# The order of five engine queues: paced by hand in the program, or recorded first and set by a list schedule

## The chip, the cores and the metric

One core of one Trainium2 chip runs the whole program. The metric is the device time of one execution in microseconds (us); lower is better. A program on one core is timed in several executions, and the median is given.

## The reference

Two transformer layers and one second block work on 512 tokens of width 1024, all in float32. Cut to what matters:

```python
for l in range(DEPTH):                       # 2 layers
    mod = silu(c) @ w_ada[l] + b_ada[l]      # shifts, scales, gates
    h = rms_norm(x, norm_mix[l]) * (1 + sc1) + sh1
    proj = h @ w_in[l]
    # delta rule: conv of 4 taps, silu, 8 heads of 128, chunks of tokens:
    #   solve (I + L) X = [v, k], then a scan over the chunks
    # window attention: 16 query heads on 2 key heads, blocks of 128 tokens
    merged = sigmoid(gate_a) * (o_dn @ w_dn_out[l]) + sigmoid(gate_b) * (o_swa @ w_swa_out[l])
    x = x + gt1 * (merged @ w_o[l])
    h = rms_norm(x, norm_ffn[l]) * (1 + sc2) + sh2
    a, b = split(h @ w_up[l])
    x = x + gt2 * ((silu(causal_dwconv(a)) * b) @ w_down[l])
# second block: band attention, a state space model, gates, a last norm
```

## The kernel before

**Products.** Each large product (`gemm_f`, `gemm_t`) reads its weights in chunks of 512 KB by SyncE's queue into `raw` (L238, three buffers). `split` makes a high part `whi` on ScalarE (L127) and a low part `wlo` on VectorE (L116), and TensorE multiplies three times in fp32r: high by high, high by low, low by high. These products write PSUM tiles named `gf` (features on partitions) or `gt` (tokens on partitions), of which there are four. A product is one matmul of 128x512.

**Chains.** Beside the products run chains of small steps with many waits between engines. A delta chain (`delta_chain`, one for each pair of heads, four in a layer) starts from `gram`, the products of keys with keys and queries, which VectorE scales into `ua`. `substitute` inverts the blocks of 16: SyncE writes `nd` to DRAM in eight DMAs, reads `pn`, VectorE runs 15 steps of a product `xt` and a sum `xi`, and the result goes out as `xd` and comes back as `xq` on other partitions. `inverse` builds the larger blocks with small matmuls on TensorE (`yps`, `zps`, `wps`) and VectorE's updates of `xf` and `wf`. A scan over four chunks follows (`kqs`, `xps`, `osps`; the state is `st`), and `delta_out` transposes the output (`otr`). A window chain (`swa_chain`, two in a layer) makes keys (`ktr`), queries (`qtr`), scores (`sc`), transposed weights (`ptr`) and values (`pvo`). `conv` runs a causal convolution on VectorE (`cacc`), whose result `qk` is transposed on TensorE (`qktr`). Part of the products by masks (`um`, `rg`) runs on GpSimd, named POOL. The second block has band chains and a state space chain of the same kind.

**What sets the order.** The chains are generators. After each three matmuls of a product `tick` adds to a credit, and for each PACE = 4 of credit `stage` advances the first chain by one step. Fixed numbers of empty steps hold a chain back until other engines are done: GAP = 6 after the substitution, OGAP = 8 before the output, WGAP, SGAP and BGAP in the others.

```python
def tick(self, n):
    self.credit += n
    while self.credit >= self.pace:
        self.credit -= self.pace
        self.stage()
```

`SEQ` names the order of a layer's parts: `F0 C0 F1 Z0 O0 C1 F2 ...`, with F for a pair's products, C for its chain, Z for gates, O for the output, Q and W for the window attention. The builder then orders what is written once more by its own rules, and hands out buffers in that order. Each engine runs its queue in order; a wait at the head holds all that stands behind.

Of the kernel before, what the change touches and what calls it, by code (L numbers as in the profile page):

```python
# [23 lines left out]
# matrix products of the gemms per stage of a chain, and the stages a chain waits for results of the other engines  # L24
PACE = 4
GAP = 6
OGAP = 8
WGAP = 1
SGAP = 7
BGAP = 3  # L30
# the order of a mixing layer's parts: delta rule heads by pairs (F products, C chain, Z gates, O output),
# window attention by key heads (Q queries, W attention)
# [7 lines left out]
# columns of the packed constants  # L40
# [4 lines left out]
# columns of the second block's packed per-feature vectors  # L45
W_GB, W_BG, W_D, W_AR, W_AI, W_DT, W_NG, W_N = 0, 16, 24, 28, 44, 60, 76, 84
# columns of a layer's packed per-feature vectors
# [4 lines left out]
# packed rows of a layer  # L52
R_QN, R_KN, R_SINK, R_ALOG, R_DTB, R_N = 0, 64, 128, 144, 152, 160


class Net:
    def __init__(self, ctx, tc, io, dbg=None):
        self.tc, self.nc, self.io, self.dbg = tc, tc.nc, io, dbg or {}
        nc = tc.nc
        self.V, self.A, self.G, self.PE, self.SP = nc.vector, nc.scalar, nc.gpsimd, nc.tensor, nc.sync  # L60
# [20 lines left out]
        self.sides = []  # L81
        self.chains, self.credit, self.pace = [], 0, PACE
# [124 lines left out]
    def rsqrt(self, out, x, n, scale, eps, name, on_pool=False):  # L207
        """out = (x * scale + eps) ** -0.5, out [128, n]"""
# [22 lines left out]
    def chunk(self, parts, kk, n, eng=None):  # L231
        """rows of kk x 128, n columns from the parts (dram views [kk * 128, n_i])"""
        raw = self.p_raw.tile([128, 1024], F32, name="raw", tag="raw")
        v = raw[:, :kk * n].rearrange("p (k c) -> p k c", k=kk)
        o = 0
        for w in parts:
            c = w.shape[1]
            self.SP.dma_start(out=v[:, :, o:o + c], in_=w.rearrange("(k p) c -> p k c", p=128))  # L238
            o += c
        hi, lo = self.split(raw, kk * n, eng)  # L240
        self.step()
        return self.views(hi, lo, kk, n)
# [6 lines left out]
    def gemm_f(self, w, c0, act, consume, ntile=2, parts=None, split=False):  # L249
        """features on partitions: tiles of 128 columns of w from c0; act: list of (hi, lo) [128, 512];  # L250
        split: the tokens' first half first"""
        kt = len(act)
        for g in range(ntile // 2):
# [11 lines left out]
            def mms(k0, n, hi, lo, ts):  # L265
                for ct in range(2):
                    o = slice(ct * 128, ct * 128 + 128)
                    for k in range(n):
# [4 lines left out]
                        self.tick(3)  # L273
# [12 lines left out]
    def gemm_t(self, parts, act, consume, step=2, last=2):  # L286
        """tokens on partitions: all columns of the parts (dram views [K, n_i]); act as in gemm_f;
        last: how many of the loads are gone through tile by tile"""
# [5 lines left out]
        def mms(t, k0, m, hi, lo):  # L294
            o = slice(t * 128, t * 128 + 128)
            for k in range(m):
# [4 lines left out]
                self.tick(3)  # L301
# [36 lines left out]
    def chain(self, gen, side=False):  # L338
        """a chain that runs after the ones before it; side: beside them"""
        (self.sides if side else self.chains).append(gen)  # L340

    def advance(self, gens, gen):
        with self.on("x"):
            try:
                next(gen)
            except StopIteration:
                gens.remove(gen)

    def stage(self):
        if self.chains:  # L350
            self.advance(self.chains, self.chains[0])
        for g in list(self.sides):
            self.advance(self.sides, g)

    def tick(self, n):
        self.credit += n
        while self.credit >= self.pace:
            self.credit -= self.pace
            self.stage()

    def flush(self):
        while self.chains or self.sides:
            self.stage()

# [1 line left out]
    def ada_acc(self, l, part):  # L366
        """sums over the rows of w_ada, still by partitions"""
# [12 lines left out]
    def ada_col(self, l, part, acc, q):  # L380
        """half q of the part as a column per 128 features: shifts, and norm * (1 + scale)"""
# [18 lines left out]
    def mod_gate(self, l, part):  # L400
        """a gate's row to dram (the first times a fourth)"""
# [15 lines left out]
    def row(self, name, src, lane="x"):  # L417
        """a row of dram on all partitions"""
# [13 lines left out]
    def norm_scale(self, ss):  # L432
        """1 / rms, a column, from both halves' sums of squares over D"""
# [5 lines left out]
    def norm_half(self, xn, t, q, a, b, h):  # L439
        """half q of the features of the scaled rows xn [128, 512], times a plus b, as hi and lo of h"""  # L440
# [24 lines left out]
    def first_norm(self, x0):  # L465
        """the modulation and norm before the first layer, a quarter of the features after the other"""
# [11 lines left out]
        def apply(q, acc):  # L478
# [3 lines left out]
            for part in range(2):  # L482
# [3 lines left out]
            self.tc.keep_in_program_order(  # L486
                self.tt(d, ps, self.vec[:, 0, V_ADA:V_ADA + 16].rearrange("p (a k) -> p a k", a=2)[:, :, f2], ADD))
# [45 lines left out]
    def conv(self, l, ps, ti, out):  # L533
        """causal conv of 4 taps along tokens, then 2 * silu"""
# [10 lines left out]
    def dn_scalars(self, l, hact):  # L545
        """k, v of the window attention and the delta rule's decays and betas"""
# [47 lines left out]
    def decays(self, b):  # L594
        """between the tokens of a chunk"""
# [14 lines left out]
    def delta_front(self, l, b, hact):  # L610
        """heads 2b, 2b + 1"""
# [52 lines left out]
        # v, token-major and scaled  # L664
# [27 lines left out]
    def delta_chain(self, l, b, qk, ua, kd, vk, sig):  # L692
        dn = self.dn
        xq = self.substitute(ua)
        for _ in range(GAP):
            yield
        tt_ = yield from self.inverse(ua, xq)
        # scan over the chunks
# [60 lines left out]
    def delta_out(self, l, b, ot, sz, odn):  # L759
        for _ in range(OGAP):  # L760
            yield
# [932 lines left out]
```

## Time and profile before

| | us |
|---|---|
| three runs | 2508.03, 2505.99, 2504.11 |
| median | 2505.99 |
| span of the profiled execution, first to last instruction | 2505.6 |
| TensorE busy in it | 2390.4 |
| VectorE, ScalarE, POOL busy | 1675.6, 1019.1, 520.1 |

The profile gives one time for the profiled execution, its span. In it PE is TensorE's matmuls and PEld its weight loads, DVE is VectorE, ACT ScalarE, SP SyncE. A matmul's end is modelled, so the distance from start to start of two matmuls tells more of the pace than the duration of one. The granted clock is a share of 2.4 GHz.

### The profile page before, as it was taken

What the parts mean: (1) busy time and instruction counts of PE and PEld (TensorE: products, weight loads), DVE (VectorE), ACT (ScalarE), POOL (GpSimd) and SP (SyncE); (2) the same over time, 40 slices, a digit from 0 to 9 for tenths busy, and PEclk for the clock granted to TensorE, in tenths of its full rate; (3) what the DMA queues carried; (4) which work ended last, traced back from release to release, by engine and by line L of the source; (5) the groups of instructions that cost most, each with busy time, mean ns of one, the idle gap of its engine ahead of it and who ended that gap; (6) DMA issues with size and microseconds to landing.
All of it is one profiled execution on the core that took longest, in us unless ns stands there. A gap on an engine that the chain in (4) does not pass through costs nothing.

```text
span 2505.6 us, 35740 instructions
## 1 busy us (share of the span) xinstructions
PE 2390.4 (95%) x13324; PEld 1939.6 (77%) x13324; DVE 1675.6 (67%) x3078; ACT 1019.1 (41%) x2095; POOL 520.1 (21%) x738
## 2 busy tenths in 40 slices
PE   6899898999999999999998989999999999999998
PEld 5677676778888888787777767888888888877786
DVE  6787788766576667478877976356646655855554
ACT  5444353642253233364434535234332334255432
POOL 2321314210500000113213241041005341600000
PEclk9999999999999999999999999999999999999999
DMA  8222223356365556442222223345533344632242
GB/s 260 71 64 63 70 72 100 118 173 223 122 202 172 171 172 196 131 125 72 57 63 64 78 70 114 112 146 179 157 113 114 103 140 156 204 115 76 82 137 76
DMA packets 239741, 309.09 MB, mean 123 GB/s; under 512 B 32144, under 2 KB 189712, under 8 KB 239568
## 3 DMA queue, kind: packets, MB, share of 16 engines
q1 hardware_dynamic: 228864, 275.64, 36.1%
q0 software_dynamic: 10416, 30.91, 3.5%
q8 instruction: 105, 1.72, 0.3%
q14 instruction: 68, 0.56, 0.1%
q10 hardware_dynamic: 288, 0.26, 0.0%
HBM read 276.20 MB, written 30.56 MB: 122 GB/s over the span
## 4 chain that ended last, share of the span: by engine, by line
PE 64%; DVE 7%; ACT 2%; issue 2%; DMA 2%; POOL 1%; SPq 0%; DVEq 0%; POOLq 0%; ACTq 0%
PE gf L130 41%; PE gt L130 15%; DVE wlo L116 1%; DVE xt L116 1%; ACT whi L127 1%; DMA raw<-in_w_ada_dram 1%; DVE cacc L119 1%; PE pvo L130 1%; PE bo L130 1%; PE sc L130 0%; DVE xi L788 0%; PE osps L130 0%; PE bs L130 0%; PE gram L130 0%; PE ntr L133 0%
## 5 line engine op out<-in xcount | busy, mean ns | idle before, releaser
L130 PE MATMUL gf<-hhi,whi 128*128 128x512 f32 (+1 forms) x1888 | 728.7, 387 | 5.1 <-ACT hhi L127 3.2
L130 PE MATMUL gf<-hlo,whi 128*128 128x512 f32 (+1 forms) x1888 | 725.7, 385 | 2.7 <-DVE hlo L116 2.7
L130 PE MATMUL gf<-hhi,wlo 128*128 128x512 f32 (+1 forms) x1888 | 724.5, 384 | 0.7 <-DVE wlo L116 0.6
L116 DVE TENSOR_TENSOR wlo<-raw,whi 128x1024 fp32r<-128x1024 f32 (+1 forms) x358 | 462.1, 1291 | 314.7 <-ACT whi L127 313.1
L127 ACT ACTIVATE whi<-raw 128x1024 fp32r<-128x1024 f32 (+1 forms) x366 | 378.3, 1036 | 631.2 <-PE gf L130 290.5
L130 PEld LDWEIGHTS gf<-hhi,whi 128*128 128x128 f32 x1888 | 359.7, 191 | 68.1 <-ACT hhi L127 4.0
L130 PEld LDWEIGHTS gf<-hlo,whi 128*128 128x128 f32 x1888 | 360.5, 191 | 62.8 <-DVE hlo L116 4.3
L130 PEld LDWEIGHTS gf<-hhi,wlo 128*128 128x128 f32 x1888 | 360.4, 191 | 62.0 <-DVE wlo L116 2.0
L130 PE MATMUL gt<-whi,g 128*128 128x512 f32 x704 | 219.5, 392 | 0.0
L130 PE MATMUL gt<-whi,hhi 128*128 128x512 f32 (+1 forms) x416 | 158.3, 381 | 5.0 <-ACT beta L127 2.7
L130 PE MATMUL gt<-whi,hlo 128*128 128x512 f32 (+1 forms) x416 | 157.6, 379 | 0.0
L130 PE MATMUL gt<-wlo,hhi 128*128 128x512 f32 (+1 forms) x416 | 157.5, 379 | 0.0
L130 PEld LDWEIGHTS gt<-whi,g 128*128 128x128 f32 x704 | 132.3, 189 | 27.2 <-issue 0.2
L130 PE MATMUL gt<-wlo,g 128*128 128x512 f32 x352 | 137.7, 391 | 0.0
L119 DVE SCALAR_TENSOR_TENSOR acc<-raw,csil,acc 128x1024 f32<-128x1024 f32 x70 | 89.7, 1281 | 60.1 <-DMA raw<-in_w_ada_dram 59.8
L119 DVE SCALAR_TENSOR_TENSOR cacc<-gf,vec,cacc 128x511 f32<-128x511 f32 x144 | 106.8, 742 | 33.8 <-ACT cacc L127 32.6
L130 PE MATMUL gf<-rhi,whi 128*128 128x512 f32 x256 | 99.8, 390 | 0.0
L130 PE MATMUL gf<-rhi,wlo 128*128 128x512 f32 x256 | 99.6, 389 | 0.0
L130 PE MATMUL gf<-rlo,whi 128*128 128x512 f32 x256 | 99.6, 389 | 0.0
L130 PEld LDWEIGHTS gt<-whi,hhi 128*128 128x128 f32 x416 | 78.5, 189 | 19.4 <-ACT beta L127 3.4
L119 DVE SCALAR_TENSOR_TENSOR facc<-gf,vec,facc 128x511 f32<-128x511 f32 x88 | 65.8, 747 | 36.5 <-ACT facc L127 35.2
L130 PEld LDWEIGHTS gt<-whi,hlo 128*128 128x128 f32 x416 | 78.5, 189 | 14.2 <-issue 0.8
(414 smaller groups left out, 3610.6 us busy)
## 6 DMA issues: line engine op xcount, KB each, us to landing
raw<-in_w_in_dram SPq DMA_DIRECT2D x140, 512.0 KB, 3.7
raw<-in_w_ada_dram SPq DMA_DIRECT2D x80, 512.0 KB, 3.9
raw<-in_w_up_dram SPq DMA_DIRECT2D x80, 512.0 KB, 4.1
raw<-in_w_down_dram SPq DMA_DIRECT2D x40, 512.0 KB, 3.7
wa<-in_w_ada_dram SPq DMA_DIRECT2D x32, 256.0 KB, 6.0
raw<-in_w_dn_out_dram SPq DMA_DIRECT2D x16, 512.0 KB, 3.5
raw<-in_w_swa_out_dram SPq DMA_DIRECT2D x16, 512.0 KB, 4.6
raw<-in_w_o_dram SPq DMA_DIRECT2D x16, 512.0 KB, 3.6
```

What stands on the lines that cost most here:

```text
L116: return (eng or self.V).tensor_tensor(out=out, in0=a, in1=b, op=op)
L119: return self.V.scalar_tensor_tensor(out=out, in0=a, scalar=s, in1=b, op0=op0, op1=op1)
L127: return self.A.activation(out, a, f, **kw)
L130: return self.PE.matmul(out, l, r, start=start, stop=stop)
```

## The change

The program is no longer built as it is written. Every engine is wrapped, so that each call becomes a record with a cost from a formula. All chains are recorded in one go at the place where they are started, and the credit, the stages and the empty steps are gone. `plan` then runs a list schedule over the five queues: at each turn it takes the engine that can start first, and there, of the records whose inputs and buffers are ready by the formulas, the one that was recorded first. A buffer's turns go in the recorded order. `emit` builds the instructions in the planned order and ties each to the one before it on its engine, and the first uses of a tag's buffers to each other, by edges that cost no semaphore. The instructions themselves and their shapes are the same.

```diff
-PACE = 4
-GAP = 6
-OGAP = 8
-WGAP = 1
-SGAP = 7
-BGAP = 3
...
+PE_HZ, GAP_R, GAP_F = 2.39, 13.0, 4.0
...
+class Eng:
...
+    def __getattr__(self, name):
+        f = getattr(self._eng, name)
+        return lambda *a, **k: self._rec.add(self._key, name, f, a, k)
...
+        if name == "dma_start":
+            n = max(free_of(out) * out.ap[0][1], 1) * 4
+            return (700 if key == POOL_E else 60), n
+        if key == PE_E:
+            r, l = ins[1], ins[0]
+            n = free_of(r)
+            if name == "transpose":
+                return 109 if l.dtype == F32 else 84, 0
+            if r.dtype == F32R:
+                return n / PE_HZ + GAP_R, 0
...
+        if key == ACT_E:
+            return 175 + 0.87 * n + (200 if k.get("accum_out") is not None else 0), 0
...
+            return 330 + 2.1 * n, 0
+        if name in ("tensor_tensor", "scalar_tensor_tensor", "copy_predicated", "tensor_reduce", "transpose", "select"):
+            return 110 + 1.16 * n, 0
...
+        o.tail = 170 if key == PE_E else 60
...
+        o.prio = o.n + self.bias
...
+                if turn[tag] != k or not freed[tag]:
+                    parked.setdefault(tag, {}).setdefault(k, []).append(o)
+                    return
+                since[tag, k] = t = heapq.heappop(freed[tag])
+                turn[tag] += 1
...
+        while count < len(ops):
+            best = None
+            for e in engines:
+                t = clock[e]
+                if avail[e]:
+                    s = t
+                elif future[e]:
+                    s = max(t, future[e][0][0])
+                else:
+                    continue
+                if best is None or s < best[0]:
+                    best = (s, e)
+            if best is None:
+                raise RuntimeError("no plan: slots %s" % {g: (turn[g], len(order[g]), sorted(parked.get(g, {}))[:3]) for g in turn if parked.get(g)})
+            s, e = best
+            fe, av = future[e], avail[e]
+            while fe and fe[0][0] <= s:
+                r, p, n = heapq.heappop(fe)
+                heapq.heappush(av, (p, n))
+            p, n = heapq.heappop(av)
+            o = ops[n]
+            o.start = s
+            d = o.dur
+            if e == PE_E:
+                if o.mode != mode:
+                    d += 110
+                    mode = o.mode
+            end = s + d
...
+                done = max(dma_free, end) + (2300 if e == SP_E else 2600)
...
+    def emit(self, seq):
+
+        info = mybir.DependencyInfo(mybir.DependencyClass.NoSync, mybir.DependencyReason.DATA)
+        last, seen = {}, set()
+        for o in seq:
+            f, a, k = o.call
+            i = f(*a, **k).ins
+            after = [o.eng]
+            for t in o.tiles:
+                if t.name not in seen:
+                    seen.add(t.name)
+                    after.append("slots " + t.tag)
+            for p in dict.fromkeys(last[g] for g in after if g in last):
+                self.tc.add_manual_dep(i, p, info, reason="plan")
+            for g in after:
+                last[g] = i.name
...
+        rec = self.rec = Recorder(tc)
+        self.V, self.A, self.G = rec.engine(DVE_E, nc.vector), rec.engine(ACT_E, nc.scalar), rec.engine(POOL_E, nc.gpsimd)
+        self.PE, self.SP = rec.engine(PE_E, nc.tensor), rec.engine(SP_E, nc.sync)
...
-                        self.tick(3)
...
     def chain(self, gen, side=False):
-        """a chain that runs after the ones before it; side: beside them"""
-        (self.sides if side else self.chains).append(gen)
-
-    def advance(self, gens, gen):
         with self.on("x"):
-            try:
-                next(gen)
-            except StopIteration:
-                gens.remove(gen)
-
-    def stage(self):
-        if self.chains:
-            self.advance(self.chains, self.chains[0])
-        for g in list(self.sides):
-            self.advance(self.sides, g)
-
-    def tick(self, n):
-        self.credit += n
-        while self.credit >= self.pace:
-            self.credit -= self.pace
-            self.stage()
+            for _ in gen:
+                pass
...
     def delta_chain(self, l, b, qk, ua, kd, vk, sig):
         dn = self.dn
         xq = self.substitute(ua)
-        for _ in range(GAP):
-            yield
         tt_ = yield from self.inverse(ua, xq)
...
+    n.rec.emit(n.rec.plan())
```

Three places show how the built order moves. The first is TensorE in the first layer, where the inverse of the first pair of heads begins. `yps` and `zps` are its first small matmuls, of 32x32. Before:

```order
L130 MATMUL gf<-hhi,whi 128x512
L130 MATMUL yps<-xf,um 32x32 x32
L130 MATMUL gf<-hlo,whi 128x512
L130 MATMUL gf<-hhi,wlo 128x512
L130 MATMUL gf<-hhi,whi 128x512
L130 MATMUL zps<-y_1116,wf 32x32 x32
```

And now:

```order
L312 MATMUL gf<-hlo,whi 128x512
L312 MATMUL yps<-xf,um 32x32 x16
L312 MATMUL gf<-hhi,wlo 128x512
L312 MATMUL yps<-xf,um 32x32 x16
L312 MATMUL gf<-hhi,whi 128x512
L312 MATMUL gf<-hlo,whi 128x512
L312 MATMUL gf<-hhi,wlo 128x512
L312 MATMUL zps<-y_327,wf 32x32 x32
```

The group of `yps` is cut in two around a product, and three products stand before `zps` as they did. The group as a whole comes sooner after the pair's last `gram`: 94 instructions of TensorE lie between them now, 135 did before.

The second place is VectorE in the same layer, near the end of the substitution of the last pair, beside a window chain (`sden`, `pp`) and the norm of queries (`rnm`, `rni`, `rrs`). Before:

```order
L116 TENSOR_TENSOR xt<-xi,pn 64x10x10
L124 TENSOR_SCALAR rnm<-rss 128x16
L788 TENSOR_REDUCE xi<-xt 64x10
L116 TENSOR_TENSOR sden<-sden,ses 128x8
L123 TENSOR_SCALAR rni<-rnm 128x16
L116 TENSOR_TENSOR xt<-xi,pn 64x11x11
L990 RECIPROCAL sden<-sden 128x8
L788 TENSOR_REDUCE xi<-xt 64x11
L116 TENSOR_TENSOR pp<-pp,sden 128x512
L116 TENSOR_TENSOR xt<-xi,pn 64x12x12
L124 TENSOR_SCALAR rrs<-rni 128x16
L788 TENSOR_REDUCE xi<-xt 64x12
```

And now:

```order
L312 TENSOR_TENSOR xt<-xi,pn 64x12x12
L312 TENSOR_REDUCE xi<-xt 64x12
L312 TENSOR_TENSOR xt<-xi,pn 64x13x13
L312 TENSOR_REDUCE xi<-xt 64x13
L312 TENSOR_TENSOR xt<-xi,pn 64x14x14
L312 TENSOR_REDUCE xi<-xt 64x14
L312 TENSOR_TENSOR xt<-xi,pn 64x15x15
L312 TENSOR_REDUCE xi<-xt 64x15
L312 TENSOR_TENSOR wlo<-raw,whi 128x1024 x3
L312 TENSOR_REDUCE rss<-rsq 128x16
```

The steps of the substitution now follow each other, and the weights' splits and the queries' norm come behind them. In the other seven chains they stand in the same way, with a few foreign steps between them in some.

The third place is SyncE in the first layer, around the first substitution's DMAs. Before:

```order
L238 DMA raw<-in_w_in_dram 128x4x256 x4
L778 DMA nd<-ua 16x8x16 x8
L238 DMA raw<-in_w_in_dram 128x4x256
L780 DMA pn<-nd 64x256
L238 DMA raw<-in_w_in_dram 128x4x256 x3
L790 DMA xd<-xi 64x256
L792 DMA xq<-xd 128x8x16
```

And now:

```order
L312 DMA raw<-in_w_in_dram 128x4x256 x4
L312 DMA nd<-ua 16x8x16 x8
L312 DMA pn<-nd 64x256
L312 DMA raw<-in_w_in_dram 128x4x256
L312 DMA xd<-xi 64x256
L312 DMA xq<-xd 128x8x16
```

`pn` is read ahead of the next weight load, and one load stands before `xd` where four did between `nd` and `xd`.

## Rows read from the trace of the kernel before

**Rows 1.** The page: span, and busy time of each engine.
```profile
span 2505.6 us, 35740 instructions
...
PE 2390.4 (95%) x13324; PEld 1939.6 (77%) x13324; DVE 1675.6 (67%) x3078; ACT 1019.1 (41%) x2095; POOL 520.1 (21%) x738
```

**Rows 2.** Stages: length; busy us (instructions) PE, PEld, DVE, ACT, POOL; clock, DMA, GB/s.
```profile
0.00:58.00 58.00, 36.71 (x160) 28.86 (x160) 41.81 (x74) 30.79 (x52) 12.92 (x17) 1.00 0.83 258
58.00:545.00 487.00, 445.49 (x3010) 347.06 (x3010) 387.30 (x941) 224.70 (x621) 132.78 (x139) 0.96 0.31 90
545.00:1080.00 535.00, 527.55 (x2472) 438.74 (x2470) 335.15 (x418) 183.14 (x252) 58.91 (x109) 1.00 0.55 173
1080.00:1550.00 470.00, 440.39 (x3086) 350.68 (x3086) 368.02 (x889) 220.73 (x608) 123.13 (x123) 0.97 0.27 78
1550.00:2112.00 562.00, 556.92 (x2637) 461.10 (x2636) 312.77 (x394) 199.28 (x296) 144.86 (x298) 0.99 0.42 135
2112.00:2505.60 393.60, 383.38 (x1967) 313.15 (x1965) 230.55 (x366) 160.45 (x267) 47.53 (x53) 0.99 0.36 115
```

**Rows 3.** The same view of 50 us among the second layer's output products.
```profile
1600.00:1650.00 50.00, 50.00 (x222) 41.42 (x221) 23.77 (x26) 15.12 (x15) 0.00 (x0) 1.00 0.53 179
```

**Rows 4.** Waits of PE, 58:545: us in total, times, longest.
```profile
PE yps L130 <- DVE xf L116: 8.3, 4, 5.9
PE ktr L133 <- ACT kst L127: 6.4, 2, 3.9
PE qktr L133 <- DVE qk L119: 6.4, 4, 4.5
PE kqs L130 <- DVE st L119: 3.9, 1, 3.9
```

**Rows 5.** Waits of PE, 1080:1550.
```profile
PE yps L130 <- DVE xf L116: 9.5, 4, 4.1
PE qktr L133 <- DVE qk L119: 6.1, 3, 5.3
PE ktr L133 <- ACT kst L127: 5.2, 2, 2.7
```

**Rows 6.** Timeline of SP, one substitution: start, us, issue.
```profile
1279.32 3.64 SPq L778 DMA_DIRECT2D nd<-ua  x8
...
1284.10 0.46 SPq L780 DMA_DIRECT2D pn<-nd  x1
...
1300.70 0.46 SPq L790 DMA_DIRECT2D xd<-xi  x1
...
1302.63 0.37 SPq L792 DMA_DIRECT2D xq<-xd  x1
```

**Rows 7.** Timeline of DVE and PE around it: start, us, instruction [idle before].
```profile
1277.56 1.74 DVE L119 SCALAR_TENSOR_TENSOR ua<-gram,sj,em 128x256 f32<-128x256 f32 x4 [0.54 <-PE gram L130]
...
1306.13 2.21 DVE L116 TENSOR_TENSOR xf<-xq,cst 128x512 f32<-128x512 f32 x2 [4.38 <-DMA xq<-xd]
...
1307.89 0.55 PE L130 MATMUL yps<-xf,um 128*32 128x32 f32 x24 [2.92 <-DVE xf L116]
```

**Rows 8.** Windows of the eight substitutions, xt's instructions alone: length, DVE busy.
```profile
1290.60:1300.70 10.10, 7.93 (x30) 1.00 0.37 105
...
sum 130.10, DVE 72.91; mean DVE 9.11
```

**Rows 9.** Timeline of POOL, DVE and PE in the first layer's chains.
```profile
292.70 1.90 POOL L116 TENSOR_TENSOR rg<-cst,glo 128x1024 fp32r<-128x1024 f32 x1
292.81 1.82 DVE L116 TENSOR_TENSOR rnt<-rrs 128x16 f32<-128x16 f32 x1
...
295.48 0.17 DVE L116 TENSOR_TENSOR rnt<-rrs 128x16 f32<-128x16 f32 x1
...
296.68 0.63 PE L130 MATMUL kqs<-st,qk 128*128 128x128 f32 x2 [3.87 <-DVE st L119]
```

More of the change, by code (lines that the diff above doesn't have):

```diff
@@ L53, with __init__ @@
 R_QN, R_KN, R_SINK, R_ALOG, R_DTB, R_N = 0, 64, 128, 144, 152, 160
+PE_HZ, GAP_R, GAP_F = 2.39, 13.0, 4.0
+DVE_E, ACT_E, POOL_E, SP_E, PE_E = "DVE", "ACT", "POOL", "SP", "PE"
+class Op:
+    __slots__ = ("n", "eng", "name", "call", "dur", "tail", "dep", "succ", "left", "ready", "tiles", "need", "prio", "start", "mode", "bytes")
+class Eng:
+    def __init__(self, rec, key, eng):
+        self._rec, self._key, self._eng = rec, key, eng
+    def __getattr__(self, name):
+        f = getattr(self._eng, name)
+        return lambda *a, **k: self._rec.add(self._key, name, f, a, k)
@@ L59, in __init__ @@
         nc = tc.nc
-        self.V, self.A, self.G, self.PE, self.SP = nc.vector, nc.scalar, nc.gpsimd, nc.tensor, nc.sync
+        rec = self.rec = Recorder(tc)
+        self.V, self.A, self.G = rec.engine(DVE_E, nc.vector), rec.engine(ACT_E, nc.scalar), rec.engine(POOL_E, nc.gpsimd)
+        self.PE, self.SP = rec.engine(PE_E, nc.tensor), rec.engine(SP_E, nc.sync)
         def pool(name, bufs, **kw):
@@ L80, in __init__ @@
         self.hold, self.pre = 0, {}
-        self.sides = []
-        self.chains, self.credit, self.pace = [], 0, PACE
         self.psg = pool("psg", 4, space=bass.MemoryType.PSUM)
@@ L300, in mms @@
                 self.mm(ps[t][:, :n], al[:, o], hi[:, k], start=False, stop=k0 + k == kt - 1)
-                self.tick(3)
         held = []
@@ L338, in chain @@
     def chain(self, gen, side=False):
-        (self.sides if side else self.chains).append(gen)
-    def advance(self, gens, gen):
         with self.on("x"):
-            try:
-                next(gen)
-            except StopIteration:
-                gens.remove(gen)
-    def stage(self):
-        if self.chains:
-            self.advance(self.chains, self.chains[0])
-        for g in list(self.sides):
-            self.advance(self.sides, g)
-    def tick(self, n):
-        self.credit += n
-        while self.credit >= self.pace:
-            self.credit -= self.pace
-            self.stage()
+            for _ in gen:
+                pass
     def flush(self):
-        while self.chains or self.sides:
-            self.stage()
+        pass
     def ada_acc(self, l, part):
@@ L485, in apply @@
             d = self.modc[:, 0, 0, :, f2]
-            self.tc.keep_in_program_order(
-                self.tt(d, ps, self.vec[:, 0, V_ADA:V_ADA + 16].rearrange("p (a k) -> p a k", a=2)[:, :, f2], ADD))
+            self.tt(d, ps, self.vec[:, 0, V_ADA:V_ADA + 16].rearrange("p (a k) -> p a k", a=2)[:, :, f2], ADD)
             d = d[:, 1]
@@ L759, in delta_out @@
     def delta_out(self, l, b, ot, sz, odn):
-        for _ in range(OGAP):
-            yield
         for h in range(2):
@@ L993, in swa_chain @@
                 self.tt(p[:, h], p[:, h], den[:, h].unsqueeze(2).broadcast_to([128, 4, 128]), MUL, e)
-            for _ in range(WGAP):
-                yield
             pc = self.b4("pc", (128, 8, 128))
@@ L1423, in ssm @@
                 st[n] = states(n)
-                for _ in range(SGAP):
-                    yield
             if n:
                 outputs(n - 1, *st.pop(n - 1))
-                for _ in range(SGAP):
-                    yield
+            yield
     def band_front(self, j, hact):
@@ L1482, in band_chain @@
             pts = []
-            for _ in range(BGAP):
-                yield
             for p in ps:
```

170 lines of the change are left out of this document (added).

## The prediction

> **What bounds the kernel now.** I read the head of the page first. TensorE is busy for 2390.4 of 2505.6 us [rows 1], so it is the engine to shorten, and only 115.2 us of it are idle. The next view, busy time by stage, tells where [rows 2]. I cut the span at the start, the first layer's chains, its output products and FFN, the same two for the second layer, and the second block. TensorE stands idle for 58.00 - 36.71 = 21.3 us at the start, 487.00 - 445.49 = 41.5 us in the first chains, 7.5 us after them, 470.00 - 440.39 = 29.6 us in the second chains, then 5.1 and 10.2 us. The two chain stages hold 71.1 of the 115.2 us. They also have a lower granted clock, 0.96 and 0.97, where the FFN stage has 1.00: (1 - 0.96) x 487 = 19.5 us and (1 - 0.97) x 470 = 14.1 us, together 33.6 us, in which the array ran at 1.2 GHz in place of 2.4. So what an order can give back in the chains is about 71.1 + 33.6 = 104.7 us.
>
> Outside them little can be had. In a stretch of the output products TensorE is busy throughout, with 222 products in 50 us, 0.225 us each [rows 3]; this is the price that I use for a product. VectorE is busy 387.30 of 487 us (80%) and 368.02 of 470 us (78%) in the chain stages [rows 2]. It is the second bound: if TensorE's waits all went, the first chain stage would last some 487 - 41.5 - 19.5 = 426 us, and VectorE's 387 us would then be 91% of it. An engine that full can only just keep up.
>
> The view of waits names what TensorE waits for in the chain stages: the first products of the inverse (yps) 8.3 and 9.5 us, the transposed keys (ktr) 6.4 and 5.2, the transposes after the convolution (qktr) 6.4 and 6.1, and single ones such as kqs, 3.9 [rows 4, 5]. All but ktr are released by VectorE.
>
> **The change part by part.** No instruction is added or taken away; both built programs hold 11822 matmuls. What changes is who stands before whom. The fixed distances (PACE, GAP and the like) go, and each chain instruction stands where the planner's own costs say that its input is just ready. At the inverse of the first pair both orders put three products between yps and zps, so a single chain step gains nothing; where the whole chain stands has moved.
>
> *The inverse, yps (17.8 us of the idle time).* What must pass between the last gram and the first yps is a run of small DMAs and VectorE steps. In one chain of the second layer its parts show: ua begins at 1277.56, eight nd writes are issued from 1279.32, pn is read from 1284.10, xd is written at 1300.70, xq read from 1302.63, xf begins at 1306.13 and yps at 1307.89 [rows 6, 7]. From the end of ua (1277.56 + 1.74 = 1279.30) that is 28.6 us, with the shortest of the eight substitutions (a 10.1 us window with 7.93 us busy, against a mean of 130.10 / 8 = 16.3 us) [rows 8]. As the change leaves the substitution almost undivided on VectorE (its order shows that), I take 10 us for each, and 29 us for the whole way. In the new order 94, 132, 145, 134 instructions of TensorE stand between gram and yps in the first layer's four pairs and 117, 145, 147, 134 in the second's. Priced at 0.225 us, which is an upper bound as some are shorter, they cover 21.2, 29.7, 32.6, 30.2 and 26.3, 32.6, 33.1, 30.2 us. So the first pair of each layer waits, 29 - 21 = 8 and 29 - 26 = 3 us, and I add 1 us for the two last pairs. That is 12 us where 17.8 were: a gain of 6. The planner does not see it: by its costs in the diff the substitution takes 2 x (15 x 0.11 + 1.16 x 1.24) = 6.2 us (1240 is the sum of the squares to 15) and the eight nd issues 0.5 us, where rows show 10.1 and 3.64.
>
> *The other waits (71.1 - 17.8 = 53.3 us).* No row of the kernel before shows how these end under the new order. One bound is that all go, since products are at hand as a filler in every pair; the other is that all stay. I take two thirds as gone, 35 us, nearer to the first, because most waits are on chains that the new order merely puts later or earlier by some us. The third that stays is of the kind that no plan foresees. One such is in the rows: a VectorE step on 128x16 took 1.82 us while a POOL product of 1.90 us ran, and 0.17 us later with POOL off; kqs, whose state update is queued behind it, then waited 3.87 us [rows 9].
>
> The Trainium skill (SBUF — State Buffer, section "SBUF: two separate sides") says that VectorE and GpSimd share one port pair as an exclusive lock, which also a VectorE instruction with two SBUF inputs takes, and that the loser blocks for the whole instruction. The trace agrees, with the 1.82 us of [rows 9]. By that rule the sum would lose up to what the last rival below prices; by the rows alone I keep the third.
>
> *The clock (33.6 us).* The clock is 1.00 where TensorE hardly waits and 0.96 and 0.97 in the two stages with the waits [rows 2]. I let its loss shrink with the idle time: (6 + 35) / 71.1 = 58% of 33.6 is 19 us. Bounds are nothing and all of it.
>
> *What stays.* The FFN's products stand in the same order as before, and I take nothing from the start, which runs at 258 GB/s with the DMA engines busy 0.83 [rows 2], or from the second block, whose waits are 10.2 us in all. VectorE's and ScalarE's work is off the path there. The weight loads on SyncE keep their sequence but for single steps past the small DMAs; a product group stays at hand, so no price.
>
> *Sum.* 6 + 35 + 19 = 60 us. From the profiled execution's 2505.6 us that gives 2445.6; the median of the three runs is 2505.99, so I predict 2446 us.
>
> **The rivals.** *More than this: nearly all of the chains' loss goes.* Only the 12 us at yps stay: 71.1 - 12 + 33.6 = 92.7 us, so 2413 us. For it speaks that a product is ready nearly always; against it VectorE at 91%.
>
> *The waits only move.* Each wait goes and another takes its place, since the builder had already mixed several chains finely on VectorE, and yps shows that even a full plan leaves 12 of 17.8 us. Then the time is 2506 us. Against it: ktr and qktr wait for work that a plan can put earlier.
>
> *Slower: the planned margins are too thin.* In a chain, about 22 steps of each of the eight delta chains and 20 of each of the four window chains, 256 in all, stand just in time. Whenever a POOL instruction holds up VectorE, the step is late by 1.82 - 0.17 = 1.65 us [rows 9], TensorE waits, and the weight splits queued behind on VectorE come late too. POOL is busy 132.78 of 487 us, 27% [rows 2], so at most 0.27 x 256 x 1.65 = 114 us. Where the 60 us of gain are eaten, after 36 such steps, it turns; with 90 us of such lateness the time is 2506 - 60 + 90 = 2536 us. For it: the planner knows no lock, prices substitution and nd 7 us short per chain, and has dropped every fixed distance. Against it: each stop of TensorE lets the other engines catch up, so that two late steps seldom cost double, and the kernel before already pays for such meetings within its 71.1 us.
>
> **How the numbers follow.** The forecast has 0.57, the larger gain 0.15, moved waits 0.08, the slower rival 0.20. If all of the other waits go or only a third does, that is 18 us either way, and with them goes 18 / 71.1 = 25% of the clock's 33.6 us, 8 us; rounded up for the clock's own bounds, the forecast's own range is 2415 to 2480. The range reaches down to 2400 (92.7 us and a little of the start) and up to 2520, into the slower rival, whose part beyond that is about 0.13; below 2400 I leave 0.04. About 0.2% (5 us) is what a measurement can tell from no change. Faster by more than that: 0.57 + 0.15 = 0.72. Within it: 0.08. Slower: 0.20.
>
> **What would show it.** Right: in the new profile the two stretches up to each layer's output products are shorter by 25 to 35 us each, the FFN stretches are the same, products still come at 222 in 50 us, yps of the first pair waits some 8 us for xf, and the substitution's windows are 10 to 11 us. The clock in the chains is 0.98 or more. Wrong: many short waits of TensorE for VectorE steps, each beside a POOL instruction (the slower rival); a chain stage of old length with VectorE near 95% (VectorE is the bound); waits for whi or wlo in front of plain products (the weight pipe starves).

## The result: 2.7% slower, and the profile after

The changed kernel takes 2575.36 us (median of four runs, 2573.59 to 2578.57) where the kernel before takes 2507.01 us: a ratio of 1.0274, 95% interval 1.0259 to 1.0288. The prediction was 2446 us, with a range to 2520. The head of its page answers to [rows 1]:

```profile
span 2572.5 us, 35800 instructions
...
PE 2409.9 (94%) x13324; PEld 1956.1 (76%) x13324; DVE 1707.2 (66%) x3078; ACT 1023.7 (40%) x2093; POOL 531.9 (21%) x738
```

TensorE is idle for 2572.5 - 2409.9 = 162.6 us where it was 115.2, and busy for 19.5 us more with the same products. The view of cores gives a mean granted clock of 0.975, before 0.984. To compare stages, both spans are cut where the same work begins: at the first output product (gf<-rhi) of a layer, at the first product on the normed rows (gf<-hhi) after them, and at the first one after the FFN's last product. Columns as in [rows 2]; first the kernel before:

```profile
0.00:563.30 563.30, 500.49 (x3250) 391.05 (x3251) 435.26 (x1019) 260.95 (x680) 146.50 (x157) 0.97 0.37 110
563.30:699.80 136.50, 134.91 (x614) 111.66 (x612) 82.47 (x108) 44.59 (x63) 37.84 (x72) 1.00 0.53 174
699.80:1079.80 380.00, 374.14 (x1777) 311.76 (x1777) 246.33 (x306) 132.89 (x183) 20.27 (x36) 1.00 0.55 172
1079.80:1594.50 514.70, 484.77 (x3291) 384.44 (x3291) 386.19 (x921) 235.33 (x640) 127.39 (x128) 0.97 0.28 80
...
2104.40:2505.60 401.20, 390.73 (x2015) 320.29 (x2013) 236.91 (x379) 165.22 (x278) 49.97 (x56) 0.99 0.37 117
```

The changed kernel, the same stages:

```profile
0.00:579.00 579.00, 505.57 (x3250) 397.80 (x3251) 457.36 (x1019) 262.31 (x678) 146.51 (x157) 0.95 0.36 106
579.00:720.90 141.90, 135.85 (x614) 111.43 (x613) 85.37 (x109) 45.93 (x66) 38.19 (x72) 1.00 0.53 174
720.90:1106.30 385.40, 376.78 (x1772) 313.02 (x1772) 246.16 (x302) 131.32 (x179) 20.57 (x36) 0.99 0.54 168
1106.30:1634.20 527.90, 484.25 (x3295) 387.28 (x3296) 400.29 (x924) 239.31 (x642) 134.71 (x128) 0.97 0.27 78
...
2148.30:2572.50 424.20, 399.96 (x2016) 325.04 (x2016) 240.75 (x381) 164.79 (x279) 49.34 (x56) 0.98 0.35 110
```

The first stage is 15.7 us longer, then 5.4 and 5.4, the second layer's chains 13.2, the two stages left out 1.1 and 3.1, the second block 23.0 us: 66.9 us. The chains, where the gain was to come from, lose 29 us, the second block nearly as much. The view of waits (us in total, times, longest) says for what TensorE waits now:

```profile
PE gt L312 <- DVE wlo L312: 19.3, 6, 7.1
PE ntr L312 <- ACT x L312: 14.6, 3, 13.5
PE gf L312 <- DVE wlo L312: 14.2, 4, 6.0
PE gf L312 <- ACT hhi L312: 13.1, 5, 3.8
PE ntr L312 <- DVE xn L312: 13.1, 9, 2.5
PE qktr L312 <- DVE qk L312: 13.0, 4, 5.2
PE vtr L312 <- DVE vt L312: 10.1, 5, 4.7
...
PE ktr L312 <- ACT kst L312: 1.6, 3, 1.3
```

The same view of the kernel before has other rows on top:

```profile
PE yps L130 <- DVE xf L116: 17.8, 8, 5.9
...
PE ktr L133 <- ACT kst L127: 11.7, 4, 3.9
...
PE gf L130 <- ACT hhi L127: 3.2, 2, 1.6
...
PE ntr L133 <- DVE xn L123: 2.1, 2, 2.0
...
PE gf L130 <- DVE wlo L116: 0.6, 2, 0.4
...
PE vtr L133 <- DVE vt L119: 0.2, 1, 0.2
```

yps is gone from the list and ktr nearly so. But the idle time on the way to yps is not gone; it stands before other work there. The eight stretches from a pair's last gram to its first yps, by the view of windows (length and TensorE's busy time), before and now:

```profile
sum 281.26, PE 248.85 PEld 193.60 DVE 240.59 ACT 107.38 POOL 94.37; mean PE 31.11 PEld 24.20 DVE 30.07 ACT 13.42 POOL 11.80
sum 298.71, PE 244.39 PEld 189.46 DVE 251.48 ACT 86.84 POOL 91.30; mean PE 30.55 PEld 23.68 DVE 31.43 ACT 10.86 POOL 11.41
```

TensorE's idle time in them went up from 281.26 - 248.85 = 32.4 to 298.71 - 244.39 = 54.3 us. In the first pair qktr waits, because the convolution that makes qk stands behind the substitution on VectorE:

```profile
128.99 0.38 DVE L312 TENSOR_REDUCE xi<-xt 64x15 f32<-64x225 f32 x1
...
132.64 0.68 DVE L312 SCALAR_TENSOR_TENSOR qk<-cth,cacc 128x512 f32<-128x512 f32 x1
133.38 1.12 PE L312 MATMUL qktr<-cst,qk 128*128 128x128 f32 x4 [4.99 <-DVE qk L312]
...
137.41 0.66 PE L312 MATMUL yps<-xf,um 128*32 128x32 f32 x32
```

At the head of the list stand plain products that wait for the low parts of their weights (wlo), 19.3 + 14.2 = 33.5 us where it was 0.6, with work on the norms (hhi, xn) and the values (vt) behind them. One of the longest of these waits, on VectorE and TensorE:

```profile
408.56 0.68 DVE L312 TENSOR_TENSOR pv<-ptr,cst 128x512 f32<-128x512 f32 x1
409.15 0.68 DVE L312 TENSOR_TENSOR pc<-ptr,cst 128x512 f32<-128x512 f32 x1
...
411.33 0.15 DVE L312 TENSOR_TENSOR xt<-xi,pn 64x1 f32<-64x1 f32 x1
...
415.62 0.39 PE L312 MATMUL gt<-whi,hhi 128*128 128x512 f32 x1
...
419.72 1.80 DVE L312 TENSOR_TENSOR xt<-xi,pn 64x225 f32<-64x225 f32 x1
419.86 1.26 POOL L312 TENSOR_TENSOR um<-ua,cst 128x512 f32<-128x512 f32 x1
421.05 0.53 POOL L312 MEMSET yy<- 128x512 f32 x1
421.56 0.38 DVE L312 TENSOR_REDUCE xi<-xt 64x15 f32<-64x225 f32 x1
421.86 2.34 DVE L312 TENSOR_TENSOR wlo<-raw,whi 128x1024 fp32r<-128x1024 f32 x2
423.12 0.80 PE L312 MATMUL gt<-wlo,hhi 128*128 128x512 f32 x1 [7.11 <-DVE wlo L312]
```

From 411.33 to 421.94 VectorE does the substitution and little else. TensorE's last product on split weights starts at 415.62; the next splits stand behind the substitution, and TensorE waits 7.11 us. The view of windows, of xt's instructions alone (length, VectorE busy, clock), answers to [rows 8]:

```profile
117.80:129.40 11.60, 10.57 (x30) 1.00 0.11 37
...
411.30:421.95 10.65, 9.12 (x30) 0.86 0.13 37
1191.50:1201.25 9.75, 8.72 (x30) 0.97 0.05 19
...
1472.50:1483.10 10.60, 9.09 (x30) 0.88 0.13 37
sum 103.47, DVE 78.82; mean DVE 9.85
```

Four of the eight substitutions are now blocks of 9.75 to 11.6 us, and the mean window is 103.47 / 8 = 12.9 us where it was 16.3.

The planner stores the start that it gives each instruction (o.start) and its own end (self.end), which is 2419.7 us. Its starts of some TensorE instructions, their starts in the trace, and the difference, in us:

```
planned   trace    late
   66.9    66.2    -0.6
  217.2   250.5    33.3
  420.2   485.8    65.6
  546.4   615.1    68.6
 1024.4  1088.3    63.9
 1225.6  1323.9    98.3
 1426.8  1549.0   122.2
 2005.8  2129.8   124.0
 2233.7  2380.1   146.4
 2410.1  2559.9   149.8
```

The plan holds within some 5 us where there are only products, and falls back by 68, 58 and 26 us in the two chain stages and the second block. So by its own prices the plan is faster than the kernel before; the chip doesn't keep it.

### The profile page after: what moved, and what is told of

Its sections match the earlier page's. It is cut to its first block, busy times and chain, and to the rows that moved or that the text cites. A ratio compares the mean times of both kernels' runs of the same rounds, so it can differ in the third digit from the quotient of the medians.

```text
span 2572.5 us, 35800 instructions
## 1 busy us (share of the span) xinstructions
PE 2409.9 (94%) x13324; PEld 1956.1 (76%) x13324; DVE 1707.2 (66%) x3078; ACT 1023.7 (40%) x2093; POOL 531.9 (21%) x738
## 5 line engine op out<-in xcount | busy, mean ns | idle before, releaser
L312 DVE TENSOR_TENSOR wlo<-raw,whi 128x1024 fp32r<-128x1024 f32 (+1 forms) x358 | 451.7, 1269 | 398.8 <-ACT whi L312 392.2
L312 PEld LDWEIGHTS gt<-wlo,hhi 128*128 128x128 f32 x416 | 79.7, 192 | 34.0 <-DVE wlo L312 20.4
L312 PEld LDWEIGHTS gt<-whi,hhi 128*128 128x128 f32 x416 | 79.2, 191 | 16.3 <-DVE cacc L312 1.7
```

Source lines behind the costliest of these rows:

```text
L312: i = f(*a, **k).ins
```

## The experiments

Three theories were set against each other. *Lock*: VectorE is held up by POOL's products, of which the planner knows nothing (the mechanism of the slower rival). *Costs*: the planner's prices are wrong, so what it puts just in time comes late. *Greedy*: taking whatever is ready in program order is bad at any price. Ratios are to the kernel before on the same chip.

**POOL's products taken out of both kernels.** In the changed kernel at emission (e4), in the kernel before in its helper (e5):

```diff
+            if o.eng == POOL_E and o.name == "tensor_tensor" and free_of(k["out"]) > 8:
+                w = k["out"]
+                f, a, k = o.call[0].__self__.memset, (w.bitcast(F32) if w.dtype == F32R else w, 0.0), {}
             i = f(*a, **k).ins
```

> The changed kernel in the same planned order, but each two-input POOL operation over more than 8 columns writes zeros to its output in place of the product or sum (left out: those products and sums), so that POOL is busy less and holds no two-input lock. Theory lock: the VectorE durations above their form's lower quartile, 83 us in the changed kernel, mostly go, and with them 50 to 70 us of the time: 2510 us. Theory costs and theory greedy: POOL is not the cause, 2560 us or more.

> The kernel before with the same cut as e4: each two-input POOL operation over more than 8 columns writes zeros to its output (left out: those products and sums). Theory lock as the cause of the slowdown: the hand-paced order has slack for such meetings, so it gains less than the 63 us of e4, 20 us or less, 2490 us. Theory that both orders pay the lock alike and the planner's prices make the difference: some 60 us, 2450 us.

Measured: e4 2512.14 us (1.0024, 1.0013 to 1.0036), 63 us less than the changed kernel; e5 2450.45 us (0.9779, 0.9764 to 0.9794), 56 us less than the kernel before. The pages' rows:

```profile
PE 2397.1 (95%) x13324; PEld 1952.9 (78%) x13324; DVE 1623.1 (65%) x3078; ACT 1023.1 (41%) x2093; POOL 273.1 (11%) x738
```

```profile
PE 2373.2 (97%) x13324; PEld 1930.8 (79%) x13324; DVE 1581.0 (65%) x3078; ACT 1017.1 (42%) x2093; POOL 269.4 (11%) x738
```

VectorE's same instructions are 84.1 and 94.6 us shorter (1707.2 and 1675.6 before). Taken alone, e4 met theory lock's number; e5 is the run that decides, and it met the number of its second theory. So the lock is real and dear, but both orders pay it about alike. Without POOL's products 62 us still lie between the two kernels, and the lock explains some 7 of the 68 us (in e5 the builder also orders anew, so this is no sharper). POOL's own work is shorter too in both runs, so their 63 and 56 us are not the lock's alone. In the trace of the changed kernel VectorE's durations above their form's lower quartile (by 250 ns or more) sum to some 84 us, before to 101 us, and in e4 and e5 to 7 and 14: the meetings have not become more. Theory lock falls as the reason for the slowdown.

**The planner's prices, one after the other.** e1 gives the substitution's steps and the issue of a DMA the durations of the trace; e6 all durations of VectorE, ScalarE and POOL (a table of 286 rows); e7 the spacing; e9 and e10 spacing with one of the others; e2 all.

```diff
-            return (700 if key == POOL_E else 60), n
+            return (600 if key == POOL_E else 460), n
...
+        o.dur = self.measured(key, name, out, ins, o.dur)
...
+FREE, NEXT = {DVE_E: -82, ACT_E: -95, POOL_E: -45}, {DVE_E: 34, ACT_E: 122, POOL_E: 78}
...
-            clock[e] = end
+            clock[e] = end + FREE.get(e, 0)
...
-                when = end if (q.eng == e and o.name != "dma_start") else done
+                when = end + NEXT.get(e, 0) if (q.eng == e and o.name != "dma_start") else done
```

> The changed kernel, whose planner is given the chip's durations for the steps of the substitution (pn, xt, xi; 0.53 us for the longest xt where it had 0.37) and for the issue of a DMA (0.46 us on SyncE where it had 0.06). Theory costs (the planner's prices are too low, so what it puts just in time comes late): if these two prices are the ones that matter, the eight chains give back some 5 us each and a little clock, 2525 us. Theory lock (VectorE is held up by POOL products of which the planner knows nothing): no change, 2575 us. Theory greedy (the order is bad whatever the prices, because the planner takes what is ready in program order): no change, 2575 us.

> Of e2 only the prices of single operations on VectorE, ScalarE and POOL (measured durations), with no spacing between operations of an engine and DMA issue at 0.06 us as in the changed kernel. By its own prices this plan ends at 2448 us. If wrong durations alone made the plan bad, most of the 71 us of e2 come back, 2520 us; if it is the spacing or the DMA issue, it stays at 2570 us.

> Of e2 only the spacing: what follows on the same engine comes 82, 95 or 45 ns before the end if it doesn't depend on it, 34, 122 or 78 ns after it if it does (VectorE, ScalarE, POOL); durations and DMA issue as in the changed kernel. By its own prices this plan ends at 2382 us. If the missing spacing made the plan bad, most of the 71 us of e2 come back, 2520 us; if it is the durations or the DMA issue, it stays at 2570 us.

> e6 and e7 together: measured durations and spacing, but DMA issue at 0.06 us as in the changed kernel. Theory that the prices work only together (each alone shifts the mistakes elsewhere): faster than the 2549 us of e7 by 20 us or more. If the rest of e2 (45 us) is the DMA issue: 2549 us.

> e7 with the issue of a DMA at its measured 0.46 us, durations as in the changed kernel. If the rest of e2 is the DMA issue: 2504 us; if it is the durations together with the spacing: 2549 us.

> As e1, but every operation of VectorE, ScalarE and POOL has the lower quartile of its duration in the changed kernel's trace as its price, and what follows on the same engine comes 82 (VectorE) or 95 ns (ScalarE) before its end if it doesn't depend on it, 34 or 122 ns after it if it does. By its own prices this plan ends at 2389 us. Theory costs: the 2389 us hold but for the clock and the lock, 2389 + 45 + 50 = 2485 us. Theory lock: most of the loss stays, 2550 us. Theory greedy: 2570 us.

| prices that are the chip's | us | ratio to before (95%) | wlo waits, us | planner's own end, us |
|---|---|---|---|---|
| none: the changed kernel | 2575.36 | 1.0274 (1.0259 to 1.0288) | 33.5 | 2420 |
| e1 substitution and DMA issue | 2583.22 | 1.0307 (1.0287 to 1.0327) | 29.2 | 2431 |
| e6 durations | 2582.87 | 1.0312 (1.0297 to 1.0328) | 46.3 | 2448 |
| e7 spacing | 2549.16 | 1.0177 (1.0160 to 1.0194) | 6.3 | 2382 |
| e10 spacing, DMA issue | 2544.40 | 1.0150 (1.0135 to 1.0165) | 8.3 | 2390 |
| e9 spacing, durations | 2519.13 | 1.0059 (1.0036 to 1.0081) | 1.4 | 2383 |
| e2 all three | 2503.99 | 0.9990 (0.9977 to 1.0003) | 2.3 | 2389 |

(The column of wlo adds the rows of the view of waits in which gf or gt waits for VectorE's wlo.) With all prices right the 2.7% are gone, by the same code and the same rule of choice: theory costs holds, if 19 us above its number. But e1 missed by 58 us. It corrected the two prices that the prediction had named, and nothing came back; nor did all durations alone bring anything. Spacing alone gives 26 us, between the two numbers of e7. Durations on top of it give 30, as e9's first theory has it. The DMA issue gives 15 on top of both, but only 5 on top of spacing alone (e10, near its second number). The orders of e1 and e6 differ from the changed kernel's in many places, so their 8 us more are not read as the price of anything, and steps of that size elsewhere are no sharper.

The planner's own end says something of the parts. From the profiled span less this end, the chip is behind the plan by 153 us in the changed kernel, 132 in e6, 163 in e7, 132 in e9, 114 in e2. So durations bring the chip 20 to 30 us nearer to its plan with or without spacing, but without it they also make the plan 28 us longer. Spacing makes the plan shorter by 37 us, and the chip no nearer to it. Ends by different prices are not one ruler, so this is an account and no proof.

**Why spacing comes first.** The planner lets a step start the moment the step before it on the same engine ends, whether it depends on it or not. The substitution's 30 steps are a chain in which each depends on the last, and its number in the program is low; so each is ready exactly when VectorE is free, is chosen, and the chain becomes a block. With spacing a dependent step is ready 34 ns after the end and VectorE free 82 ns ahead of it, and something else is taken in between. In e2's trace:

```profile
364.69 0.14 DVE L612 TENSOR_TENSOR xt<-xi,pn 64x1 f32<-64x1 f32 x1
364.75 1.21 DVE L612 TENSOR_TENSOR wlo<-raw,whi 128x1024 fp32r<-128x1024 f32 x1
365.89 0.14 DVE L612 TENSOR_REDUCE xi<-xt 64x1 f32<-64x1 f32 x1
...
sum 151.65, DVE 74.25; mean DVE 9.28
```

The last row is that of the eight windows: 151.65 / 8 = 19.0 us each, longer than the 12.9 us of the changed kernel and better. In e1 and e6, which gave nothing, the substitutions are still blocks: their windows are 13.4 and 12.4 us in the mean, in e7 16.5. To test this alone, e13 spaces the substitution's steps and nothing else; e14 moves the splits forward instead.

```diff
+                if q.eng == e == DVE_E and q.tiles[-1].name.split("_")[0] in ("xt", "xi"):
+                    when += 116
                 q.ready = max(q.ready, when)
```

```diff
-        o.prio = o.n + self.bias
+        o.prio = o.n + self.bias - (1000 if key in (DVE_E, ACT_E) and outs[0].tensor.name.split("_")[0] in ("whi", "wlo") else 0)
```

> The changed kernel with one price changed: a step of the substitution on VectorE (xt, xi) is planned 116 ns after the end of the step that it depends on, so that the planner finds VectorE free in between (the 30 steps then span 33 to 75 VectorE instructions of its order, where they spanned 30 to 49). Theory block (the substitution stands as one block of some 10 us on VectorE, and the weight splits behind it starve TensorE): the waits for wlo (33.5 us in the changed kernel) mostly go, with some clock, 2545 us or less. Theory that all steps of the chains are late alike and the substitution is only one of many: 2565 us or more.

> The changed kernel's prices; the weight splits (whi, wlo on ScalarE and VectorE) are taken before other ready work of a program order up to 1000 operations older. The substitution stays a block (30 steps span 31 to 42 instructions). Theory block: splits are made earlier where buffers allow, so part of the waits for wlo goes, 2555 us; if the three buffers keep the splits behind the block, 2575 us. Theory that all steps are late alike: 2575 us.

e13: 2548.51 us (1.0172, 1.0155 to 1.0189), as much as all spacing together. Its windows and its wait for wlo:

```profile
sum 169.60, DVE 80.34; mean DVE 10.04
```

```profile
PE gf L315 <- DVE wlo L315: 16.0, 5, 6.1
```

It missed theory block's number by 3.5 us. The windows are 21.2 us long in the mean, and half of the 33.5 us of waits for wlo is gone, where most were expected to go (the row for gt is down to 0.5 us); 18.2 of its 27 us come in the first layer's chains. e14: 2589.39 us (1.0330, 1.0315 to 1.0345). It met neither number: the splits hold TensorE for 1.5 us only, but yps (19.6 us) and qktr (16.0) hold it instead. So one price, that of the substitution's next step, is shown to be worth 27 of the 68 us, by an order in which the substitution is no block. That the splits behind the block carry all of it is not shown: in e14 their waits go and the kernel gets slower, so choosing the other party first is no cure.

**Where TensorE's order and the other engines' orders come from.** e8 keeps the plan's order on TensorE and SyncE alone (and that of the buffers), e11 gives a flat slack at the planner's old prices.

```diff
-            after = [o.eng]
+            after = [o.eng] if o.eng in (PE_E, SP_E) else []
```

```diff
+                if q.eng == PE_E and e != PE_E:
+                    when += 1000
                 q.ready = max(q.ready, when)
```

> The changed kernel with the planned order kept on TensorE and SyncE alone; VectorE, ScalarE and POOL are ordered by the builder's own scheduler as in the kernel before, in this program order. If the loss lies in how the plan stacks work on VectorE (weight splits behind the substitution), it goes with that order: 2520 us or less. If it lies in where the plan puts the chain steps on TensorE, it stays: 2570 us or more.

> The changed kernel's own prices, but each TensorE instruction is planned for 1 us after its input from another engine is ready. Theory that what is missing is slack, as the hand-paced distances gave it: 2530 us or less. Theory that the prices must be right, since a flat slack also moves the work of the other engines and runs TensorE dry in the plan itself (its own end goes from 2420 to 2452 us): no gain, 2575 us or more.

e8: 2636.64 us (1.0524, 1.0508 to 1.0539), on the side of its second number (2570 us or more). Its waits for wlo are 3.6 us, yet it is 61 us slower than the changed kernel, and yps heads its list with 26.1 us. So taking the planned order off the other engines is no cure, and waits for wlo can go without a gain. The builder's rules for VectorE, which serve the hand-paced kernel, do not serve TensorE's planned order: the two orders belong together. e11: 2558.11 us (1.0207, 1.0192 to 1.0222), 17 us better than the changed kernel, between its two expectations: slack hides some errors, right prices hide more.

**A planner that knows the lock, and slack in the second block.** e3 is e2 with the lock in the planner, e12 adds 1 us for the second block's chains.

```diff
+            o.lk = e in lk and o.name not in ("dma_start", "memset") and not any("PSUM" in str(x) for x in o.spaces)
+            if o.lk:
+                s = max(s, lk[POOL_E if e == DVE_E else DVE_E])
...
+            if o.lk:
+                lk[e] = end - 60
```

```diff
+                if q.eng == PE_E and e != PE_E and q.tiles[-1].name.split("_")[0] in ("bs", "bt", "bo", "syp", "sbu"):
+                    when += 1000
```

> As e2, and the planner also starts no VectorE instruction without a PSUM operand while a POOL instruction runs, nor the reverse. By its own prices this plan ends at 2407 us. Theory costs: about as e2, 2485 us. Theory lock: clearly faster than e2, by 40 us or more, 2445 us. Theory greedy: 2570 us.

> e3 (2477 us), and in the second block each TensorE instruction of the window scores, transposes, outputs and of the state space part (bs, bt, bo, sbu, syp) is planned for 1 us after its input is ready. In e3 TensorE still waits some 1 to 1.7 us before such instructions, eight times, where the kernel before has none. If the just-in-time placing with small errors is what is left there: 2467 us. If the waits only move: 2477 us.

e3: 2477.33 us (0.9886, 0.9864 to 0.9909), 27 us below e2, where 40 were expected. e12: 2469.60 us (0.9848, 0.9834 to 0.9863), 8 us below e3, within 3 us of the first theory's number. Both beat both kernels. Stage lengths, cut as above from the views of windows:

| us | before | changed | e13 | e2 | e3 | e12 |
|---|---|---|---|---|---|---|
| start and first chains | 563.3 | 579.0 | 560.8 | 539.3 | 520.7 | 524.9 |
| output products, norm | 136.5 | 141.9 | 141.1 | 144.0 | 148.9 | 147.1 |
| FFN, norm | 380.0 | 385.4 | 384.5 | 377.6 | 380.2 | 380.1 |
| second chains | 514.7 | 527.9 | 520.8 | 504.7 | 489.2 | 489.1 |
| second block | 401.2 | 424.2 | 423.8 | 424.6 | 420.5 | 413.6 |

In the chains a plan with right prices wins 34 us (e2) and, with the lock known, 68 us (e3); the prediction's 60 us lay there. Two places lose at any price. The stage of the output products and the norm stays 5 to 12 us longer (in e3 and e12 15 and 16 of the chains' TensorE instructions have moved into it), and the second block stays some 20 us longer until it is given slack: in the kernel before TensorE waits there for 0.4 us in all, in the changed kernel ten rows of waits sum to 16.3 us, in e12 four rows to 6.3 us. This is what may be left of theory greedy: what was paced loosely and hardly waited is now placed just in time. The slack of e12 wins 7 of the 20 us there; the rest stays open.

## Why the prediction was wrong

- *yps.* A wait of 12 us was left in the sum; the view has no row of it any more (its smallest is 0.2 us). That is no success of the step. For the first pair the text had 29 us from gram to yps and 8 us of waiting; the trace has 28.6 us with TensorE idle for 6.3 of them, but before qktr and vtr. The wait was priced about rightly and moved to other rows, and TensorE's idle time grew in all eight stretches.
- *The other waits.* This is the step that failed: "I take two thirds as gone, 35 us ... because most waits are on chains that the new order merely puts later or earlier". ktr's did go (11.7 to 1.6 us), but new ones came, and idle time rose by 47.4 us. The text had seen that "the change leaves the substitution almost undivided on VectorE", and counted it as a gain for yps; what stands behind a block of 10 us on that engine got no price. Under "What stays" the weight loads were put at nothing ("a product group stays at hand, so no price"): the product is at hand only when its splits are, and they cost 33.5 us of waiting. Waits for whi or wlo in front of plain products stood among the text's own signs of being wrong.
- *The clock.* It was tied to the idle time and went the wrong way with it: (1 - 0.975) x 2572.5 = 64 us against (1 - 0.984) x 2505.6 = 40 us, some 24 us lost where 19 were to be won (TensorE's busy time says 19.5). The tie is loose: e4 has 116.1 us of idle time, as the kernel before, at a clock of 0.978. And the text's 33.6 us are what the lower clock costs, not how long the array ran at 1.2 GHz; a mean of 0.96 between the two levels puts 8% of a stretch there, twice as long.
- *What stays.* The FFN's products cost nearly the same (376.78 us busy in the first layer, 374.14 before), but the second block, from which nothing was taken, lost 23.0 us, and the two stages behind the first layer's chains 5.4 each.
- *The slower rival.* It had the sign and the wrong place: priced by POOL's lock, which both kernels pay alike (e4, e5). By the rule of the Trainium skill (SBUF — State Buffer, "SBUF: two separate sides") the lock was to cost VectorE; the trace agrees, with 84 and 95 us of VectorE time, and yet the rule does not tell the two kernels apart. The rival's clause that the planner prices substitution and DMA issue short came near the cause, but missed the price that mattered first: the two named there gave nothing when they were corrected alone (e1).
- *What was right.* The plan by its own prices ends at 2419.7 us, and with right prices and the lock known the same planner gives 2477 us. The forecast described the plan; the chip did not keep to it.

Still open: why durations help by 30 us with spacing and not at all without it. The planner's ends say where (2448 us in e6, 2383 in e9). One reading fits and was not tried on its own: recorded durations of independent neighbours overlap by some 80 ns, so a table of durations without spacing takes VectorE for fuller than it is. Open too is how much of the stage with the norm is the order of the rows and how much the splits beside them.

## What to carry to other kernels

A planned order is as good as its prices, and the one that matters may not be a duration: whether a dependent step follows at once or a little later decides whether a chain becomes a block. When a chain becomes denser on an engine, price what is queued behind it, not only what waits for its end. Set the planner's own starts beside the trace before anything else: where the difference grows, the chip does not keep the plan. But the difference does not rank two plans: e7 falls 163 us behind its plan, the changed kernel 153, and e7 is the faster one.

## What the runs showed of the hardware

- A VectorE instruction that doesn't depend on the one before starts before that one's recorded end, a dependent one after it. In the rows above pc starts at 409.15 while pv ends at 409.24. Over the changed kernel's trace the median gap is some -80 ns for independent neighbours and +34 ns for dependent ones; on ScalarE dependent neighbours stand 123 ns apart. The Trainium skill (VectorE: DVE Perf Modes, "The DRAIN you can't avoid") has a case in which a semaphore after each operation costs nothing extra; here the two kinds of neighbours differ by 116 ns, and e7 and e13 show that it matters to a planner.
- The issue of a small DMA on SyncE is no 0.06 us, as the planner has it: the eight nd writes of [rows 6] take 3.64 us, 0.46 us each, and with that price set right 15 us came back on top of spacing and durations (e9 to e2), 5 on top of spacing alone (e7 to e10).
- A chain that takes longer can leave the kernel faster: the substitution's windows grow from 12.9 to 21.2 us (e13), and the kernel gets 27 us faster.
